# Byte places of the matmul operands in an fp32 encoder: high and low halves and low weights get begins of their own

## The chip, the core and the metric

The kernel runs on one core of a Trainium2 chip. The metric is the device time of one execution in microseconds (us). A run has three executions here, and their median is quoted.

## The reference

Two layers of a bidirectional encoder over 272 positions (16 learned ones and 256 tokens), width 2048, everything in float32. Per layer:

```
h = RMSNorm(x)
[q | k | v | f | ga | gf] = h @ W_in            # 1024, 256, 256, 1024, 2048, 2048 channels
attn    = GQA(rope(norm(q)), rope(norm(k)), v)  # 8 heads, 2 kv heads, bidirectional
fourier = Re(2-D DFT of f per group of 128 channels)
a = attn @ W_attn_br ; s = fourier @ W_four
x = x + (sigmoid(ga) * a + sigmoid(gf) * s) @ W_out
h2 = RMSNorm(x)
x = x + W_down(silu(dwconv3(h2 @ W_up_gate)) * (h2 @ W_up_val))   # 5632 channels
```

The output is the residual stream after two layers without the 16 learned positions.

## The kernel before, in words

Channels lie on the 128 partitions and positions along the free axis. Every float32 value is used as a high half, its value rounded to the format that TensorE multiplies, and a low half, the remainder. A product of two such values is three matmuls: high weights with the high moving half, high weights with the low moving half, and low weights with the high moving half. In `group` these are L248, L249 and L250, and they follow each other for every tile of 128 x 128 weights.

`group` makes two output tiles (`MG = 2`) of one projection. It walks over the input tiles `kt`; one chunk of weights holds four of these (`CW = 4`) for both outputs. `order` lists all chunks of the program, `load_raw` fetches them in that order from SyncE's queue, four ahead, and `split_w` makes `wh` (ScalarE, L193) and `wl` (VectorE, L196) of each. The tiles `wh` and `wl` have three buffers each. The keys of the groups say which projection is computed: f, k, v, q, ga, gf, a, s, o, then ug and uv (up, gate and value) and d (down). The pieces of norm, attention and Fourier work are generators that are stepped after every second weight tile.

The moving operands are kept in tiles with rows of 320 floats (`XP`) of which 272 are used. `xHL` holds the normed input, its high half in row 0 and its low half in row 1 of each `kt`; `qH` and `qL` hold the attention output for a; `mH` and `mL` hold the merged branches for o; `gHL` holds the inner activations of the feed-forward part for d. The begin inside the row is `X_AT`, `Q_AT` or `G_AT`, one number of floats per entry: `X_AT[l]` and `Q_AT[l]` by layer, `G_AT[l]` likewise.

In layer 0 all positions are computed (272 columns). In layer 1 the groups q, ga, gf, a, o and ug have 258 columns, and uv and d have 256, since the learned positions are not in the output (two more are there for the convolution). Where two halves of 256 columns fit into one bank of PSUM (512), high and low go through TensorE as one matmul of 512 columns (L244), and L245 is the low weights' matmul of 256 columns.

The code runs straight down, in the order of `order`; TensorE takes its matmuls in the order in which they were issued.

Of the kernel before, what the change touches and what calls it, by code (L numbers as in the profile page):

```python
# [10 lines left out]
F32 = mybir.dt.float32  # L11
F32R = mybir.dt.float32r
# [4 lines left out]
P = 128  # L17
# [3 lines left out]
T = NM + SEQ  # L21
# [3 lines left out]
NH = 8  # L25
# [7 lines left out]
CW = 4  # L33
MG = 2
FF_SPLIT = (24, 20)
PRE = 26
XP = 320
# [9 lines left out]
HC = 64  # L47
HC1 = HC + 1
TH = T // 2 + 2
X_AT, Q_AT, G_AT = (8, 24), (24, 40), (40, 48)  # L50
BLK = ((0, 16), (16, 144), (144, 272))

C_COS, C_SIN, C_MASK = 0, T, 2 * T
# [58 lines left out]
def encoder_kernel(ctx, tc, xT, params, consts, bmat, w_in, w_abr, w_four, w_f64, w_out, w_up, w_down, outT):  # L112
# [33 lines left out]
            k0 += n  # L146
    chunks = [ch for _, chs in order for ch in chs]
    folded = {i for i, k in enumerate(k for k, chs in order for _ in chs) if k[1] == "s"}
    st = {"raw": 0, "fetch": 0, "next": 0, "grp": 0}
    raws, splits, behind = {}, {}, {}  # L150
    RAW, LOOK = 4, 2
# [34 lines left out]

    def split_w(i, a, b, eng=None):
        if i not in splits:
            splits[i] = tuple(wp.tile([P, CW, MG * P], F32R, tag=t, name=f"{t}{i}") for t in ("wh", "wl"))
        h, lo = splits[i]  # L190
        r = raws[i]
        if eng is None:
            nc.scalar.copy(h[:, a:b], r[:, a:b])  # L193
        else:
            eng.tensor_copy(h[:, a:b], r[:, a:b])
        nc.vector.tensor_tensor(lo[:, a:b], r[:, a:b], h[:, a:b].bitcast(F32), op=ALU.subtract)  # L196
        if b == CW:
            del raws[i]
# [185 lines left out]
    nc.gpsimd.memset(remO, 0.0)  # L384

    def xs(k, half, lo=0, l=0):
        return xHL[:, k, half, X_AT[l] + lo:X_AT[l] + T]

    cos = cst[:, C_COS:C_COS + T]
    sin = cst[:, C_SIN:C_SIN + T]  # L390
# [58 lines left out]
    for l in range(DEPTH):  # L449
# [6 lines left out]

        with tc.tile_pool(name=f"mix{l}", bufs=1) as mp:
            x64 = mp.tile([96, TH], F32R, name="x64")
            E = mp.tile([P, NH, XP], F32, tag="q1", name="E")[:, :, 0:T]
            qL = mp.tile([P, NH, XP], F32R, name="qL")[:, :, Q_AT[l]:Q_AT[l] + T]  # L460
            AHn = 3 * 4 * T
            ALn = 8 * XP
            o1Hf = mp.tile([P, AHn], F32R, tag="aH", name="o1H")
# [233 lines left out]
            cnt = [0]  # L697
            for pn in pns:
                nc.gpsimd.memset(pn[:, 0:P], 0.0)
            qH = mp.tile([P, NH, XP], F32R, tag="q1", name="qH")[:, :, Q_AT[l]:Q_AT[l] + T]  # L700

            def q_stage(i, qp, qsq):
                kv, j = i // 2, i % 2
# [147 lines left out]
            for half in range(2):  # L851
                mH = mL = None
                for kind, i in BRANCH_ORDER[half]:
                    j = i - 4 * half
                    if kind == "ga":
                        tha[i] = gate("ga", i)
                    elif kind == "gf":
                        w64s.append(split_w64(l, i))
                        thf[i] = gate("gf", i)
                    elif kind == "s":  # L860
                        def s_evac(m, ps, th=thf[i]):
                            e, o = (mp.tile([P, TH], F32, tag=t, name=t) for t in ("se", "so"))
                            for a, p_ in ((e, ps[0]), (o, ps[1])):
                                nc.scalar.copy(a, p_[:, TH:2 * TH])
                                nc.vector.tensor_tensor(a, p_[:, :TH], a, op=ALU.add)
                            sp = mp.tile([P, T], F32, tag="sp", name="sp", bufs=2)
                            nc.vector.tensor_tensor(sp[:, 0:TH], e, o, op=ALU.add)
                            nc.vector.tensor_tensor(sp[:, TH:T], e[:, T - TH:0:-1], o[:, T - TH:0:-1], op=ALU.subtract)
                            t_ = th[:, m, lo:T]
                            nc.vector.scalar_tensor_tensor(t_, t_, 1.0, sp[:, lo:T], op0=ALU.add, op1=ALU.mult)  # L870

                        four_group((l, "s", i), fr, x64, w64s.pop(0), s_evac)
                    else:
                        if mH is None:
                            drain()
                            mHf = mp.tile([P, AHn], F32R, tag="aH", name="mH")
                            mLf = mp.tile([P, ALn], F32R, tag="aL", name="mL")
                            mH, mL = (t_[:, :8 * XP].rearrange("p (k t) -> p k t", k=8)[:, :, Q_AT[l]:Q_AT[l] + T] for t_ in (mHf, mLf))
                        ps = group((l, "a", i), lambda kt: (qH[:, kt, lo:T], qL[:, kt, lo:T]), W)
                        for m in range(MG):  # L880
                            k = 2 * j + m
                            t_, h_ = tha[i][:, m, lo:T], mH[:, k, lo:T]
                            nc.vector.scalar_tensor_tensor(t_, t_, 1.0, ps[m][:, :W], op0=ALU.add, op1=ALU.mult)
                            nc.vector.tensor_tensor(t_, t_, thf[i][:, m, lo:T], op=ALU.add)
                            nc.scalar.copy(h_, t_)
                            nc.vector.tensor_tensor(mL[:, k, lo:T], t_, h_.bitcast(F32), op=ALU.subtract)
                for mg in range(8):
                    ps = group((l, "o", half, mg), lambda kt: (mH[:, kt, lo:T], mL[:, kt, lo:T]), W)
                    for m in range(MG):
                        mt = 2 * mg + m  # L890
                        nc.vector.scalar_tensor_tensor(XT[:, mt, lo:T], ps[m][:, :W], 0.5, XT[:, mt, lo:T], op0=ALU.mult, op1=ALU.add)
                        if half == 1:
                            norm_in(mt, P_NF + l * KT)


        with tc.tile_pool(name=f"ffn{l}", bufs=1) as fp:
            hold = {}
            push(norm_stats(hold), 8)
            fused = 2 * W2 <= 512
            k0 = 0  # L900
            for c, n in enumerate(FF_SPLIT):
                gHL = fp.tile([P, FF_SPLIT[0], 2, XP], F32R, tag="gHL", name="gHL")[:, :, :, G_AT[l]:G_AT[l] + T]
                gH, gL = gHL[:, :, 0, :], gHL[:, :, 1, :]
                for i in range(k0 // MG, (k0 + n) // MG):
                    ps = group((l, "ug", i), xr(lo), W)
                    drain()
                    cs = []
                    for m in range(MG):
                        mt = 2 * i + m
                        wc = lambda t: prm[:, P_CW + (l * 3 + t) * FT + mt:P_CW + (l * 3 + t) * FT + mt + 1]  # L910
                        bc = prm[:, P_CB + l * FT + mt:P_CB + l * FT + mt + 1]
                        u = fp.tile([P, T], F32, tag="u", name="u", bufs=3)
                        nc.vector.tensor_tensor(u[:, lo:T], ps[m][:, :W], rstdB[:, lo:T], op=ALU.mult)
                        cv = fp.tile([P, T], F32, tag="cv", name="cv", bufs=4)
                        nc.scalar.activation(cv[:, lo2:T], u[:, lo2:T], AF.Identity, bias=bc, scale=wc(1))
                        a = max(lo2, 1)
                        nc.vector.scalar_tensor_tensor(cv[:, a:T], u[:, a - 1:T - 1], wc(0), cv[:, a:T], op0=ALU.mult, op1=ALU.add)
                        nc.vector.scalar_tensor_tensor(cv[:, lo2:T - 1], u[:, lo2 + 1:T], wc(2), cv[:, lo2:T - 1], op0=ALU.mult, op1=ALU.add)
                        nc.scalar.activation(cv[:, lo2:T], cv[:, lo2:T], AF.Silu)
                        nc.vector.tensor_tensor(cv[:, lo2:T], cv[:, lo2:T], rstdB[:, lo2:T], op=ALU.mult)  # L920
                        cs.append(cv)
                    ps = group((l, "uv", i), (lambda kt: (xHL[:, kt, :, X_AT[l] + lo2:X_AT[l] + T],)) if fused else xr(lo2), W2)
                    for m in range(MG):
                        j = 2 * i + m - k0
                        cv = cs[m]
                        val = ps[m][:, :W2]
                        if fused:
                            v = fp.tile([P, W2], F32, tag="v", name="v", bufs=2)
                            nc.scalar.copy(v, ps[m][:, W2:2 * W2])
                            nc.vector.tensor_tensor(v, v, val, op=ALU.add)  # L930
                            val = v
                        nc.vector.tensor_tensor(cv[:, lo2:T], cv[:, lo2:T], val, op=ALU.mult)
                        nc.scalar.copy(gH[:, j, lo2:T], cv[:, lo2:T])
                        nc.vector.tensor_tensor(gL[:, j, lo2:T], cv[:, lo2:T], gH[:, j, lo2:T].bitcast(F32), op=ALU.subtract)
                lastc = c == len(FF_SPLIT) - 1
                for mg in range(8):
                    two = fused and not (lastc and mg == 7)
                    ps = group((l, "d", c, mg), (lambda kt: (gHL[:, kt, :, lo2:T],)) if two
                               else (lambda kt: (gH[:, kt, lo2:T], gL[:, kt, lo2:T])), W2)
                    for m in range(MG):  # L940
                        mt = 2 * mg + m
# [62 lines left out]
```

## Time and profile before

| | |
|---|---|
| median of 3 executions | 2561.47 us (2561.24 to 2562.99) |
| profiled execution | 2561.68 us |
| its span, first to last instruction | 2559.8 us |
| TensorE, matmuls | 2552.6 us busy, 19732 matmuls |
| TensorE, weight loads | 2494.2 us busy |
| VectorE | 1690.4 us busy, 66% |
| ScalarE | 1211.4 us busy, 47% |
| GpSimd | 18.3 us busy |
| transfers | 465 MB, 57% of the 16 engines' time |
| granted TensorE clock | 0.999 of full |

A matmul's record reaches from its start to the end of its last column's way through the array, so records of successive matmuls overlap: their mean length is about 285 ns while a new one starts about every 120 ns. The distance between starts is read from the timeline.

### The profile page before, as it was taken

What the parts mean: (1) busy time and instruction counts of PE and PEld (TensorE: products, weight loads), DVE (VectorE), ACT (ScalarE), POOL (GpSimd) and SP (SyncE); (2) the same over time, 40 slices, a digit from 0 to 9 for tenths busy, and PEclk for the clock granted to TensorE, in tenths of its full rate; (3) what the DMA queues carried; (4) which work ended last, traced back from release to release, by engine and by line L of the source; (5) the groups of instructions that cost most, each with busy time, mean ns of one, the idle gap of its engine ahead of it and who ended that gap; (6) DMA issues with size and microseconds to landing.
All of it is one profiled execution on the core that took longest, in us unless ns stands there. A gap on an engine that the chain in (4) does not pass through costs nothing.

```text
span 2559.8 us, 47859 instructions
## 1 busy us (share of the span) xinstructions
PE 2552.6 (100%) x19732; PEld 2494.2 (97%) x19732; DVE 1690.4 (66%) x2691; ACT 1211.4 (47%) x1741; POOL 18.3 (1%) x37
## 2 busy tenths in 40 slices
PE   9999999999999999999999999999999999999999
PEld 9999999999999999999999999999999998999988
DVE  7687767766565446655566878677766665566654
ACT  6455434554444334444444555345554543455443
POOL 0000000000000000000000000000000000000000
PEclk9999999999999999999999999999999999999999
DMA  7555656555555555555554546666555556655565
GB/s 236 166 153 166 192 183 189 185 175 179 180 176 181 177 178 181 175 181 178 177 172 153 174 150 199 192 199 191 184 186 189 185 187 190 189 188 186 186 202 160
DMA packets 132011, 465.34 MB, mean 182 GB/s; under 512 B 15312, under 2 KB 19280, under 8 KB 131792
## 3 DMA queue, kind: packets, MB, share of 16 engines
q1 hardware_dynamic: 127424, 457.37, 56.5%
q10 hardware_dynamic: 4368, 4.92, 0.6%
q8 instruction: 154, 2.52, 0.4%
q14 instruction: 65, 0.53, 0.1%
HBM read 457.35 MB, written 2.10 MB: 179 GB/s over the span
## 4 chain that ended last, share of the span: by engine, by line
PE 98%; DVE 1%; DMA 0%; ACT 0%; issue 0%; SPq 0%; DVEq 0%; ACTq 0%
PE ps_ug L249 7%; PE ps_ug L248 7%; PE ps_ug L250 7%; PE ps_uv L244 6%; PE ps_d L244 6%; PE ps_d L249 4%; PE ps_d L250 4%; PE ps_d L248 4%; PE ps_uv L248 3%; PE ps_uv L249 3%; PE ps_uv L250 3%; PE ps_uv L245 3%; PE ps_d L245 3%; PE ps_o L249 2%; PE ps_o L248 2%; PE ps_gf L248 2%
## 5 line engine op out<-in xcount | busy, mean ns | idle before, releaser
L196 DVE TENSOR_TENSOR wl<-raw,wh 128x1024 fp32r<-128x1024 f32 (+1 forms) x835 | 1016.8, 1220 | 697.3 <-ACT wh L193 692.4
L193 ACT CAST wh<-raw 128x1024 fp32r<-128x1024 f32 (+1 forms) x834 | 871.3, 1047 | 994.4 <-PE ps_ug L249 159.5
L248 PE MATMUL ps_ug<-xHL,wh 128*128 128x272 f32 (+1 forms) x1408 | 399.6, 284 | 0.0
L249 PE MATMUL ps_ug<-xHL,wh 128*128 128x272 f32 (+1 forms) x1408 | 399.0, 283 | 0.0
L250 PE MATMUL ps_ug<-xHL,wl 128*128 128x272 f32 (+1 forms) x1408 | 399.0, 283 | 0.0
L248 PEld LDWEIGHTS ps_ug<-xHL,wh 128*128 128x128 f32 x1408 | 264.2, 188 | 0.9
L249 PEld LDWEIGHTS ps_ug<-xHL,wh 128*128 128x128 f32 x1408 | 264.2, 188 | 0.1
L250 PEld LDWEIGHTS ps_ug<-xHL,wl 128*128 128x128 f32 x1408 | 264.1, 188 | 0.0
L244 PE MATMUL ps_uv<-xHL,wh 128*128 128x512 f32 x704 | 245.0, 390 | 0.0
L244 PE MATMUL ps_d<-gHL,wh 128*128 128x512 f32 x664 | 230.3, 391 | 0.0
L249 PE MATMUL ps_d<-gHL,wh 128*128 128x272 f32 (+1 forms) x744 | 212.0, 285 | 0.0
L248 PE MATMUL ps_d<-gHL,wh 128*128 128x272 f32 (+1 forms) x744 | 212.0, 285 | 0.0
L250 PE MATMUL ps_d<-gHL,wl 128*128 128x272 f32 (+1 forms) x744 | 212.0, 285 | 0.0
L248 PE MATMUL ps_uv<-xHL,wh 128*128 128x272 f32 x704 | 200.6, 285 | 0.0
L249 PE MATMUL ps_uv<-xHL,wh 128*128 128x272 f32 x704 | 200.6, 285 | 0.0
L250 PE MATMUL ps_uv<-xHL,wl 128*128 128x272 f32 x704 | 200.6, 285 | 0.0
L245 PE MATMUL ps_uv<-xHL,wl 128*128 128x256 f32 x704 | 198.5, 282 | 0.0
L245 PE MATMUL ps_d<-gHL,wl 128*128 128x256 f32 x664 | 185.9, 280 | 0.0
L244 PEld LDWEIGHTS ps_uv<-xHL,wh 128*128 128x128 f32 x704 | 132.1, 188 | 26.9
L244 PEld LDWEIGHTS ps_d<-gHL,wh 128*128 128x128 f32 x664 | 124.2, 187 | 27.2
L248 PE MATMUL ps_ga<-xHL,wh 128*128 128x272 f32 (+1 forms) x512 | 147.5, 288 | 0.0
L248 PE MATMUL ps_gf<-xHL,wh 128*128 128x272 f32 (+1 forms) x512 | 146.3, 286 | 0.0
(284 smaller groups left out, 5891.7 us busy)
## 6 DMA issues: line engine op xcount, KB each, us to landing
raw<-in_w_up SPq DMA_DIRECT2D x352, 512.0 KB, 3.5
raw<-in_w_in SPq DMA_DIRECT2D x207, 512.0 KB, 3.6
raw<-in_w_down SPq DMA_DIRECT2D x176, 512.0 KB, 3.5
raw<-in_w_out SPq DMA_DIRECT2D x64, 512.0 KB, 3.5
raw<-in_w_four SPq DMA_DIRECT2D x32, 512.0 KB, 3.7
raw<-in_w_abr SPq DMA_DIRECT2D x32, 512.0 KB, 3.5
qs<-qp ACTq DMA_DIRECT2D x32, 68.0 KB, 4.1
outT<-ot ACTq DMA_DIRECT2D x16, 128.0 KB, 4.0
```

The source lines that it names most:

```text
L193: nc.scalar.copy(h[:, a:b], r[:, a:b])
L196: nc.vector.tensor_tensor(lo[:, a:b], r[:, a:b], h[:, a:b].bitcast(F32), op=ALU.subtract)
L244: nc.tensor.matmul(o2, h[:, c, sl], ab, start=kt == 0, stop=False)
L245: nc.tensor.matmul(o, lo[:, c, sl], ab[:, 0, :], start=False, stop=kt == nk - 1)
L248: nc.tensor.matmul(o, h[:, c, sl], a, start=kt == 0, stop=False)
L249: nc.tensor.matmul(o, h[:, c, sl], b, start=False, stop=False)
L250: nc.tensor.matmul(o, lo[:, c, sl], a, start=False, stop=kt == nk - 1)
```

## The change

All begins become pairs or tables. In bytes modulo 256 inside a partition, as the tiles are allocated:

| operand | before: high, low, wh, wl | after: high, low, wh, wl |
|---|---|---|
| layer 0: f, k, v, q, ga, gf, ug, uv, d | 32, 32, 128, 128 | 176, 48, 128, 192 |
| layer 0: a, o | 32, 32, 128, 128 | 240, 80, 128, 64 |
| layer 1: f, k, v | 96, 96, 128, 128 | 96, 160, 128, 160 |
| layer 1: q, ga, gf, a, o, ug (258 columns) | 152, 152, 128, 128 | 152, 216, 128, 192 |
| layer 1: uv | 160, 160, 128, 128 | 160, 224, 128, 128 |
| layer 1: d | 128, 128, 128, 128 | 192, 192, 128, 192 |

The three numbers for 258 columns are distances in the fourth row of the table: high weights from the high half 232 (128 - 152 modulo 256), low half from the high half 64, low weights from the high weights 64.

`X_AT`, `Q_AT` and `G_AT` now hold a (high, low) pair per layer. `WL_AT` gives the begin of the low weights inside a tile that is 64 floats longer. `both` builds the moving operand of the fused matmul of 512 columns: its two runs of 256 columns stand 336 floats apart for uv of layer 1 where they stood 320 apart. A tile `shift` of 128 bytes moves the tiles that follow it in the pool of the mixing part. No instruction is added, removed or moved: the order on each of TensorE, VectorE, ScalarE, GpSimd and SyncE, and the semaphore that each instruction waits for, are the same as before.

```diff
-X_AT, Q_AT, G_AT = (8, 24), (24, 40), (40, 48)
+X_AT, Q_AT, G_AT = ((44, 12), (24, 40)), ((44, 4), (8, 24)), ((12, 44), (0, 0))
+WL_AT = {(0, "a"): 48, (0, "o"): 48, (1, "d"): 16, (1, "k"): 8, (1, "v"): 8, (1, "f"): 8}
+WL_AT.update({(0, k): 16 for k in ("q", "k", "v", "f", "f01", "ga", "gf", "ug", "uv", "d")})
+WL_AT.update({(1, k): 16 for k in ("q", "ga", "gf", "a", "o", "ug")})
...
+    wl_at = [WL_AT.get(k[:2], 0) for k, chs in order for _ in chs]
...
-            splits[i] = tuple(wp.tile([P, CW, MG * P], F32R, tag=t, name=f"{t}{i}") for t in ("wh", "wl"))
+            h = wp.tile([P, CW, MG * P], F32R, tag="wh", name=f"wh{i}")
+            lo = wp.tile([P, CW * MG * P + 64], F32R, tag="wl", name=f"wl{i}")
+            o = wl_at[i]
+            splits[i] = h, lo[:, o:o + CW * MG * P].rearrange("p (c m) -> p c m", c=CW)
...
-        return xHL[:, k, half, X_AT[l] + lo:X_AT[l] + T]
+        return xHL[:, k, half, X_AT[l][half] + lo:X_AT[l][half] + T]
...
+            mp.tile([P, 32], F32, name="shift")
...
+            def both(t_, k, at):
+                a, n = at[0] + lo2, XP + at[1] - at[0]
+                if n == XP:
+                    return t_[:, k, :, a:a + W2]
+                b = 2 * XP * k + a
+                s = min(b, 2 * XP * t_.shape[1] - 2 * n)
+                return t_.rearrange("p k r n -> p (k r n)")[:, s:s + 2 * n].rearrange("p (r n) -> p r n", r=2)[:, :, b - s:b - s + W2]
...
-                gHL = fp.tile([P, FF_SPLIT[0], 2, XP], F32R, tag="gHL", name="gHL")[:, :, :, G_AT[l]:G_AT[l] + T]
-                gH, gL = gHL[:, :, 0, :], gHL[:, :, 1, :]
+                gHL = fp.tile([P, FF_SPLIT[0], 2, XP], F32R, tag="gHL", name="gHL")
+                gH, gL = (gHL[:, :, e, G_AT[l][e]:G_AT[l][e] + T] for e in range(2))
...
-                    ps = group((l, "uv", i), (lambda kt: (xHL[:, kt, :, X_AT[l] + lo2:X_AT[l] + T],)) if fused else xr(lo2), W2)
+                    ps = group((l, "uv", i), (lambda kt: (both(xHL, kt, X_AT[l]),)) if fused else xr(lo2), W2)
...
-                    ps = group((l, "d", c, mg), (lambda kt: (gHL[:, kt, :, lo2:T],)) if two
+                    ps = group((l, "d", c, mg), (lambda kt: (both(gHL, kt, G_AT[l]),)) if two
```

`qL`, `qH`, `mH` and `mL` are cut with the new pairs in the same way.

More of the change, by code (lines that the diff above doesn't have):

```diff
@@ L458, in encoder_kernel @@
             x64 = mp.tile([96, TH], F32R, name="x64")
+            mp.tile([P, 32], F32, name="shift")
             E = mp.tile([P, NH, XP], F32, tag="q1", name="E")[:, :, 0:T]
-            qL = mp.tile([P, NH, XP], F32R, name="qL")[:, :, Q_AT[l]:Q_AT[l] + T]
+            qL = mp.tile([P, NH, XP], F32R, name="qL")[:, :, Q_AT[l][1]:Q_AT[l][1] + T]
             AHn = 3 * 4 * T
@@ L699, in encoder_kernel @@
                 nc.gpsimd.memset(pn[:, 0:P], 0.0)
-            qH = mp.tile([P, NH, XP], F32R, tag="q1", name="qH")[:, :, Q_AT[l]:Q_AT[l] + T]
+            qH = mp.tile([P, NH, XP], F32R, tag="q1", name="qH")[:, :, Q_AT[l][0]:Q_AT[l][0] + T]
             def q_stage(i, qp, qsq):
@@ L877, in encoder_kernel @@
                             mLf = mp.tile([P, ALn], F32R, tag="aL", name="mL")
-                            mH, mL = (t_[:, :8 * XP].rearrange("p (k t) -> p k t", k=8)[:, :, Q_AT[l]:Q_AT[l] + T] for t_ in (mHf, mLf))
+                            mH, mL = (t_[:, :8 * XP].rearrange("p (k t) -> p k t", k=8)[:, :, o:o + T] for t_, o in zip((mHf, mLf), Q_AT[l]))
                         ps = group((l, "a", i), lambda kt: (qH[:, kt, lo:T], qL[:, kt, lo:T]), W)
```

## The prediction

> **What bounds the kernel now.** I read the page first: busy time, granted clock and the chain that ended last.
>
> ```profile
> span 2559.8 us, 47859 instructions
> PE 2552.6 (100%) x19732; PEld 2494.2 (97%) x19732; DVE 1690.4 (66%) x2691; ACT 1211.4 (47%) x1741; POOL 18.3 (1%) x37
> ...
> PEclk9999999999999999999999999999999999999999
> ...
> PE 98%; DVE 1%; DMA 0%; ACT 0%; issue 0%; SPq 0%; DVEq 0%; ACTq 0%
> ```
>
> TensorE is busy all the time at full granted clock, and 98% of the chain is its matmuls. No other engine sets the end. So the kernel's time is the number of matmuls times the distance from one start to the next. The change leaves number and shapes alone, so only that distance can move the time.
>
> Next the groups by line with shapes kept apart. Their mean duration is not the distance, since matmuls overlap, but the counts are exact.
>
> ```profile
> L244 PE MATMUL ps_uv<-xHL,wh 128*128 128x512 f32 x704 | 245.0, 390 | 0.0
> L244 PE MATMUL ps_d<-gHL,wh 128*128 128x512 f32 x664 | 230.3, 391 | 0.0
> L248 PE MATMUL ps_ug<-xHL,wh 128*128 128x272 f32 x704 | 200.9, 285 | 0.0
> L248 PE MATMUL ps_ug<-xHL,wh 128*128 128x258 f32 x704 | 198.6, 282 | 0.0
> L248 PE MATMUL ps_ga<-xHL,wh 128*128 128x272 f32 x256 | 74.4, 291 | 0.0
> ```
>
> L249 and L250 stand beside each L248 with the same count. Counted over all groups (the loops of the code give the same): layer 0 has 9984 matmuls of 272 columns (ug, uv and d 3x704 each, ga, gf and o 3x256 each, q and a 3x128 each, f 384, k and v 192 together). Layer 1 has 576 of 272 columns (f, k, v), 5184 of 258 columns (ug, ga, gf, a, o, q), 704 + 664 pairs of 512 + 256 columns (uv, d) and 120 of 256 (the last d group). That leaves 1132 others.
>
> The distances come from the timeline of PE, whose first column is the start. A down group of layer 0, 94 matmuls from the second row below to the row 871.49:
>
> ```profile
> 859.77 0.28 PE L250 MATMUL ps_d<-gHL,wl 128*128 128x272 f32 x1
> 859.89 0.29 PE L248 MATMUL ps_d<-gHL,wh 128*128 128x272 f32 x1
> ...
> 871.49 0.29 PE L249 MATMUL ps_d<-gHL,wh 128*128 128x272 f32 x1
> 871.61 0.28 PE L250 MATMUL ps_d<-gHL,wl 128*128 128x272 f32 x1
> 871.74 0.29 PE L248 MATMUL ps_d<-gHL,wh 128*128 128x272 f32 x1
> 871.86 0.28 PE L249 MATMUL ps_d<-gHL,wh 128*128 128x272 f32 x1
> 871.98 0.29 PE L250 MATMUL ps_d<-gHL,wl 128*128 128x272 f32 x1
> ```
>
> 11.60 us over 94 is 123.4 ns, in steps of 0.12 and 0.13. The same shape in layer 1, 46 matmuls of f:
>
> ```profile
> 1320.21 0.29 PE L249 MATMUL ps_f<-xHL,wh 128*128 128x272 f32 x1
> ...
> 1325.97 0.29 PE L250 MATMUL ps_f<-xHL,wl 128*128 128x272 f32 x1
> ```
>
> And 8 of v:
>
> ```profile
> 1378.91 0.29 PE L249 MATMUL ps_v<-xHL,wh 128*128 128x272 f32 x1
> ...
> 1379.92 0.29 PE L248 MATMUL ps_v<-xHL,wh 128*128 128x272 f32 x1
> ```
>
> 5.76 us over 46 is 125.2 ns, 1.01 us over 8 is 126.3 ns. Same operation, same columns, nothing waited for: what differs is where the operands begin. In bytes modulo 256 (64 columns) the moving operands begin at 32 in layer 0 and at 96 there; all weights at 128. So begins do cost time, and 1.8 ns is a difference already seen. The layer-1 shapes: gates of 258 columns, then ug (258) and uv (512 + 256).
>
> ```profile
> 1500.09 0.28 PE L250 MATMUL ps_ga<-xHL,wl 128*128 128x258 f32 x1
> ...
> 1500.57 0.28 PE L248 MATMUL ps_gf<-xHL,wh 128*128 128x258 f32 x1
> 1500.68 0.28 PE L249 MATMUL ps_gf<-xHL,wh 128*128 128x258 f32 x1
> ...
> 1501.16 0.28 PE L250 MATMUL ps_gf<-xHL,wl 128*128 128x258 f32 x1
> ```
>
> ```profile
> 1996.03 0.28 PE L249 MATMUL ps_ug<-xHL,wh 128*128 128x258 f32 x1
> ...
> 2006.59 0.28 PE L250 MATMUL ps_ug<-xHL,wl 128*128 128x258 f32 x1
> 2006.71 0.39 PE L244 MATMUL ps_uv<-xHL,wh 128*128 128x512 f32 x1
> 2006.94 0.28 PE L245 MATMUL ps_uv<-xHL,wl 128*128 128x256 f32 x1
> ...
> 2017.81 0.28 PE L248 MATMUL ps_ug<-xHL,wh 128*128 128x258 f32 x1
> ```
>
> Gates: 9 matmuls in 1.07 us, 118.9 ns, with single steps of 0.11. ug: 88 in 10.56 us, 120.0 ns, the same each time. uv: 32 pairs in 11.10 us, 346.9 ns. If the fixed part of a matmul is the same in ug and uv, 346.9 - 2 x 120.0 = 106.9 ns is the time of 252 columns, 0.424 ns each. Columns alone then are 115 ns of 272 and 109 of 258, so 8 to 11 ns of each matmul are not columns.
>
> What runs beside each matmul is the weight load of the next:
>
> ```profile
> 868.04 0.19 PEld L249 LDWEIGHTS ps_d<-gHL,wh 128*128 128x128 f32 x1
> 868.16 0.19 PEld L250 LDWEIGHTS ps_d<-gHL,wl 128*128 128x128 f32 x1
> 868.28 0.19 PEld L248 LDWEIGHTS ps_d<-gHL,wh 128*128 128x128 f32 x1
> ```
>
> One load follows the start of each matmul. I take the extra nanoseconds for collisions of the two reads, which depend on the difference of their begins. The rows show that begins matter; this cause they only suggest.
>
> The Trainium skill, SBUF — State Buffer, section "Who interferes with whom", gives TensorE two independent read ports, one for the moving operand and one for LDWEIGHTS, and says that it shares them with nobody. By that no begin changes anything and the sum is 0; the 123.4 against 125.2 ns speak against it.
>
> **The change part by part.**
>
> No instruction is added, removed or moved on any engine, and every wait is the same one. No stall goes, no queue is passed.
>
> *Layer 0, 272 columns, 9984 matmuls.* Before, all three of a tile's matmuls run beside a load whose begin is 96 above the moving one (128 - 32). After, the main projections have high 176, low 48, high weights 128, low weights 192: during the high matmuls the load of high weights is 208 above, during the low one the load of low weights 144 above. The a and o groups get 144 and 240. No row shows these differences. Bound below: all at the shorter of the two steps seen, 0.12: -3.4 ns x 9984 = -34 us. Bound above: the row nearest in place is ug, with 232: its 120.0 ns and 14 columns more at 0.424 give 125.9 ns, +2.5 ns x 9984 = +25 us; layer 1's v has the same shape at 126.3 ns, +2.9 ns, +29 us. I take half of the way down, 121.7 ns, -1.7 x 9984 = -17 us. Reason: equal steps 88 times running in ug, and the strict 0.12/0.13 turn of layer 0, show that a matmul meets the collision of the one before it again as long as the three have one difference; with two differences in turn the one that collides no longer repeats each time. It is a choice inside the bounds.
>
> *Layer 1 f, k, v, 576 matmuls.* The difference 32 remains for the high ones, becomes 0 for the low. From 125.2 (f) and 126.3 (v) to layer 0's 123.4: -2 to -3 ns, -1 us. Ends -3 (120) and +1 us.
>
> *258 columns, 5184 matmuls.* The difference is 128 - 152 = 232 before. After it is 232 for the high ones and 192 - 216 = 232 for the low: unchanged in every matmul. Low halves and low weights only move together by 64. I take 0. Ends: all at the 0.11 of the gates' shortest step, -8.9 ns x 3072 - 10 x 2112 = -48 us if it were held each time (it is two of nine steps now, and I give a quarter, -12 us, to the range); gates at ug's 120.0, +1.1 x 3072 = +3 us.
>
> *Pairs, 1368.* The high run of uv stays at 160, the low one goes to 224; d goes from 128 to 192 with its low weights at 192. uv and d differ by 32 bytes in begin now and by 1 ns in duration (390, 391). I take 0, and as ends half the step of 6 to 10 ns between 0.12 and 0.13, +-5 ns x 1368 = +-7 us.
>
> *The rest.* The mix pool moves by 128 bytes, half of the 256 that I count by. 512 of the 1132 other matmuls are the Fourier branch's:
>
> ```profile
> L283 PE MATMUL ps_s<-fr,wh 128*128 128x276 f32 x256 | 63.6, 334 | 0.0
> L284 PE MATMUL ps_s<-fr,wl 128*128 128x138 f32 x256 | 58.4, 228 | 0.4 <-DVE wl L196 0.4
> ...
> L196 DVE TENSOR_TENSOR wl<-raw,wh 128x1024 fp32r<-128x1024 f32 (+1 forms) x835 | 1016.8, 1220 | 697.3 <-ACT wh L193 692.4
> ```
>
> Taken at 0; ends 3 ns each way on 1132, +-3 us. VectorE writes the low weights at another begin; it is idle a third of the time and ends in time but for 0.4 us, so even some ns on each of its 835 writes stay covered. If that cover went, 10 ns each would be 8 us.
>
> Sum: -17 - 1 + 0 + 0 = -18 us against the profiled execution's 2561.68 us (span 2559.8 and 1.9 around it), which is 0.2 us above the median of 2561.47. The forecast is 2543.5 us.
>
> The Trainium skill, TensorE: Matmul & The Clock Gate, section "Back-to-back issue gap", gives an isolated warm gap of N/2.4 + 2.5 ns, 115.8 ns at 272 columns. The rows have 123.4; if the begins now freed every layer-0 matmul to that figure, the sum would be -76 us, an estimate from that page and no end of my range.
>
> **The rivals.**
>
> *Layer 0 is worse (slower).* The new differences collide in each matmul, as in layer 1's f and v. Price: from +1.8 ns (125.2) to +2.9 (126.3), +18 to +29 us, 2580 to 2591 us; with the bad ends of the others 2600. For it: of five groups read above, layer 0 has the least left over per column time (123.4 - 115.3 = 8.1 ns against 9.5 to 11), so a new place draws from worse ones. Against: its steps already show 0.12 and 0.13 in turn, so the good half exists. It decides from 0.5 ns on layer 0 (5 us).
>
> *No effect.* Begins matter only through the state that a stretch falls into, and the mean over all places is alike: within 5 us of 2561.5. For it: 258 columns keep their differences, d and uv are alike at two begins. Against: 123.4 and 125.2. The skill's rule of independent ports would give this too.
>
> *Much better.* Layer 0 all at 0.12 and 258 columns partly at 0.11: -34 - 12 - 3 = -49 us, 2512 us. For it: both steps occur. Against: nowhere are they held.
>
> **How the numbers follow.** A measurement here tells about 0.2%, 5 us. Chances: forecast (gain of 5 to 35 us) 0.42, much better 0.08, no effect 0.13, slower 0.37. So faster 0.50, same 0.13, slower 0.37. Predicted time 2543 us. Cases of both signs hold much of the chance; the forecast's own range is 2527 to 2556. The range reaches to the much better case at 2507 (2512 and 5 us of the pairs) and into the slower one to 2595 (above 2591, short of all bad ends).
>
> **What would show it.** In the changed trace, the start distances of layer 0's ug, uv and d: about 121.7 ns for the forecast, 125 to 126 for the slower rival, 123.4 for no effect. 258 columns stay at 119 to 120, pairs at 347. Split at 1320 us, where layer 1's f begins, the gain lies in layer 0 alone. A shift of some us in the 258 columns would break the rule that only the difference counts; a new wait of PE for VectorE would break the cover.

## The result, and the profile after

| | before | after |
|---|---|---|
| median of four executions | 2562.18 us (2561.24 to 2562.99) | 2530.70 us (2529.67 to 2531.18) |
| span of the profiled execution | 2559.8 us | 2529.3 us |
| ratio after to before | | 0.9877, 95% interval 0.9860 to 0.9894 |

The change makes the kernel faster by 31.5 us, 1.2%. The forecast was 2543 us, 18 us faster. (The median before has risen from 2561.47 us because a fourth execution, of 2562.89 us, is now counted in.) The page after shows the same picture as before, shorter:

```profile
span 2529.3 us, 47859 instructions
...
PE 2520.4 (100%) x19732; PEld 2462.1 (97%) x19732; DVE 1688.8 (67%) x2691; ACT 1211.1 (48%) x1741; POOL 18.3 (1%) x37
...
PE 98%; DVE 1%; ACT 0%; DMA 0%; issue 0%; SPq 0%; DVEq 0%; ACTq 0%
```

TensorE has as many matmuls, is still busy all the time, and is busy for 32.2 us less. The distances between starts are shorter. First where layer 1 begins (the first f row), in the timeline of before and then of after:

```profile
1308.58 0.29 PE L250 MATMUL ps_d<-gHL,wl 128*128 128x272 f32 x1
1308.71 0.29 PE L248 MATMUL ps_f<-xHL,wh 128*128 128x272 f32 x1
```

```profile
1299.40 0.28 PE L257 MATMUL ps_d<-gHL,wl 128*128 128x272 f32 x1
1299.52 0.29 PE L255 MATMUL ps_f<-xHL,wh 128*128 128x272 f32 x1
```

Layer 0 is 9.2 us shorter. Of the span's 30.5 us, 21.3 lie in layer 1. (The prediction put the border at 1320 us, which is inside that first f group.) Now the distances after, from the timeline: a down group of layer 0 (144 distances from the first to the last row), a ug group (96 from its first row to the uv row), the uv group behind it (32 pairs), and the down pairs of layer 1 (49 pairs).

```profile
870.16 0.29 PE L255 MATMUL ps_d<-gHL,wh 128*128 128x272 f32 x1
...
887.76 0.29 PE L255 MATMUL ps_d<-gHL,wh 128*128 128x272 f32 x1
...
1908.05 0.29 PE L255 MATMUL ps_ug<-xHL,wh 128*128 128x258 f32 x1
...
1919.07 0.28 PE L257 MATMUL ps_ug<-xHL,wl 128*128 128x258 f32 x1
1919.18 0.39 PE L251 MATMUL ps_uv<-xHL,wh 128*128 128x512 f32 x1
...
1930.28 0.29 PE L255 MATMUL ps_ug<-xHL,wh 128*128 128x258 f32 x1
...
2123.18 0.39 PE L251 MATMUL ps_d<-gHL,wh 128*128 128x512 f32 x1
...
2139.84 0.39 PE L251 MATMUL ps_d<-gHL,wh 128*128 128x512 f32 x1
```

The same 49 down pairs before:

```profile
2146.32 0.39 PE L244 MATMUL ps_d<-gHL,wh 128*128 128x512 f32 x1
...
2163.30 0.39 PE L244 MATMUL ps_d<-gHL,wh 128*128 128x512 f32 x1
```

Layer 0 stands at 122.2 ns (123.4 before), ug at 115.9 (120.0), uv at 346.9 (346.9), the down pairs at 340.0 (346.5). The distances from each start to the next, added up over both whole traces:

| part | matmuls | before, mean ns | after, mean ns | us |
|---|---|---|---|---|
| layer 0, 272 columns (without the first two groups) | 9792 | 123.3 to 130.8 by projection | 122.2 to 129.9 | -10.6 |
| layer 1, ug, 258 columns | 2112 | 120.1 | 116.1 | -8.3 |
| layer 1, q, ga, gf, a, o, 258 columns | 3072 | 118.7 to 121.2 | 115.6 to 119.1 | -8.3 |
| layer 1, d, pairs and the last group | 664 pairs, 120 | 347.2 | 340.7 | -4.7 |
| layer 1, uv pairs | 704 pairs | 346.7 | 346.7 | 0 |
| layer 1, f, k, v | 576 | 127.4 to 132.5 | 125.5 to 131.9 | -1.0 |
| first two groups and Fourier groups, both layers | 736 | | | +2.5 |

The means include the waits at a group's begin. The two d values are sums of the means of the two matmuls.

### The profile page after: what moved, and what is told of

The parts are those of the page before. It is cut to its first block, busy times and chain, and to the rows that moved or that the text cites. A ratio compares the mean times of both kernels' runs of the same rounds, so it can differ in the third digit from the quotient of the medians.

```text
span 2529.3 us, 47859 instructions
## 1 busy us (share of the span) xinstructions
PE 2520.4 (100%) x19732; PEld 2462.1 (97%) x19732; DVE 1688.8 (67%) x2691; ACT 1211.1 (48%) x1741; POOL 18.3 (1%) x37
## 4 chain that ended last, share of the span: by engine, by line
PE 98%; DVE 1%; ACT 0%; DMA 0%; issue 0%; SPq 0%; DVEq 0%; ACTq 0%
PE ps_ug L255 7%; PE ps_ug L257 7%; PE ps_ug L256 7%; PE ps_uv L251 6%; PE ps_d L251 6%; PE ps_d L257 4%; PE ps_d L255 4%; PE ps_d L256 4%; PE ps_uv L257 3%; PE ps_uv L255 3%; PE ps_uv L256 3%; PE ps_uv L252 3%; PE ps_d L252 3%; PE ps_o L255 2%; PE ps_gf L255 2%; PE ps_o L257 2%
## 5 line engine op out<-in xcount | busy, mean ns | idle before, releaser
L203 DVE TENSOR_TENSOR wl<-raw,wh 128x1024 fp32r<-128x1024 f32 (+1 forms) x835 | 1016.6, 1220 | 675.3 <-ACT wh L200 668.9
L251 PEld LDWEIGHTS ps_uv<-xHL,wh 128*128 128x128 f32 x704 | 131.9, 187 | 27.2
L251 PEld LDWEIGHTS ps_d<-gHL,wh 128*128 128x128 f32 x664 | 124.6, 188 | 26.1
```

The costliest lines, as they stand in the source:

```text
L251: nc.tensor.matmul(o2, h[:, c, sl], ab, start=kt == 0, stop=False)
```

## The experiments

I give places as in the change: three numbers, weights minus high half, low half minus high half, low weights minus high weights, modulo 256 bytes. Times of kernels that compute the encoder are medians of four or five executions, with seven or eight of the kernel before beside them; each kernel with TensorE alone was executed once. Before, layer 0 is 96, 0, 0 and the 258 columns 232, 0, 0; after, 208, 128, 64 (a and o: 144, 96, 192) and 232, 64, 64.

**Each layer alone.**

```diff
 # e1_layer0
-X_AT, Q_AT, G_AT = ((44, 12), (24, 40)), ((44, 4), (8, 24)), ((12, 44), (0, 0))
+X_AT, Q_AT, G_AT = ((44, 12), (24, 24)), ((44, 4), (40, 40)), ((12, 44), (48, 48))
 # no WL_AT entries of layer 1; "shift" in layer 0 alone
 # e2_layer1
+X_AT, Q_AT, G_AT = ((8, 8), (24, 40)), ((24, 24), (8, 24)), ((40, 40), (0, 0))
 # no WL_AT entries of layer 0; "shift" in layer 1 alone
```

> Only layer 0 has the new begins; layer 1 is as before. If the two layers' gains are separate (the start distances fell by 1.1 ns on layer 0's 9984 matmuls of 272 columns): about 11 us faster than before, less 2 us that the Fourier and first groups lost, so 2551 to 2554 us, layer 0 at 122.2 ns, layer 1's ug at 120.0 and uv at 346.7 ns as before. Rival, that the phase in which layer 0 leaves TensorE carries over into layer 1 (a running phase was seen to outlive waits): layer 1's 258 columns fall below 120 here too and the time is nearer 2540.

> Only layer 1 has the new begins; layer 0 is as before. Separate gains: 258 columns at 116 to 117 ns (-16 us), d pairs -5 us, f, k, v -1 us: 2539 to 2542 us, layer 0 at 123.4. Rival, carry-over from layer 0: layer 1 stays at 120 in part and the time is above 2548. By the rule of my prediction (only the difference of the two operands read at the same time counts) 258 columns would stay at 119 to 120 and the time would be 2555; the trace after already speaks against that.

Layer 0 alone: 2551.80 us beside 2561.28, ratio 0.9963 (0.9949 to 0.9977), -9.5 us. Layer 1 alone: 2540.86, ratio 0.9920 (0.9906 to 0.9935), -20.4 us. Together -29.9 where the whole change has -31.5. The border of the layers in the timelines, layer 0 alone first, then layer 1 alone:

```profile
1298.62 0.29 PE L254 MATMUL ps_f<-xHL,wh 128*128 128x272 f32 x1
```

```profile
1307.93 0.29 PE L254 MATMUL ps_f<-xHL,wh 128*128 128x272 f32 x1
```

In the first, layer 1's ug stays at 120.1 ns on the mean of the trace; in the second, layer 0's ug stays at 123.5 and layer 1's has 116.1. The gains are separate, and the rival of a phase carried over from layer 0 falls.

**The low weights back at their old place.**

```diff
-WL_AT = {(0, "a"): 48, (0, "o"): 48, (1, "d"): 16, ...}
+WL_AT = {}
 # and without both WL_AT.update lines
```

> High and low moving halves as in the changed kernel, all low weights at the old place. If it is the place of the moving halves alone that counts (the low half's own place): 2531 us kept, 258 columns at 116. If the low half and the low weights must move together, so that the difference stays 232 in 258 columns: ug goes back to 119 to 122 ns, layer 0 to 123 to 126, and the time is 2550 to 2590 us.

2587.75 us, ratio to before 1.0104 (1.0089 to 1.0119): 57 us slower than the whole change and 26 slower than no change. A ug group of its timeline, 96 starts:

```profile
1946.08 0.28 PE L253 MATMUL ps_ug<-xHL,wh 128*128 128x258 f32 x1
...
1957.78 0.40 PE L249 MATMUL ps_uv<-xHL,wh 128*128 128x512 f32 x1
```

That is 121.9 ns. Layer 0's ug has 124.6, the d pairs 353. At these places, moving the halves without the low weights is a loss; the moves gain only together. The numbers lie in the second of the two expected ranges. Whether its reason holds, that the difference of the two reads must stay, is tested next.

**TensorE alone.** The kernel here keeps two tiles of weights and one of moving data in place and issues stretches of the same three matmuls with begins from a table. No other engine works while they run, and the transfers are down to 1 GB/s.

```diff
+    for g, ci in enumerate(SEQUENCE):
+        kind, n, hi, lo, wh, wl = COMBOS[ci]
...
+                    nc.tensor.matmul(p[:, :n], h, a, start=kt == 0, stop=False)
+                    nc.tensor.matmul(p[:, :n], h, b, start=False, stop=False)
+                    nc.tensor.matmul(p[:, :n], l, a, start=False, stop=kt == KTN - 1)
```

> TensorE alone: 357 stretches of 48 matmuls (or 16 pairs) with operands at given byte places, each of 119 combinations three times in a shuffled order; no projection is computed and the output is not the reference's. If the extra time comes from TensorE's own two reads, the distances repeat those of the kernels within 1 ns: 272 columns with all moving at 32 and weights at 128: 123.4; 258 columns at 152: 118.7 to 120; with low half and low weights moved by 64: 116; pairs of uv 346.7, of d 346.7 before and 340.7 after; and moving all four places by the same bytes changes nothing. If it takes the other engines' or the transfers' traffic, the distances come out nearer to the columns alone, 115 and 109 ns, and no longer depend on the places.

```profile
PE 2091.6 (99%) x16560; PEld 2066.2 (98%) x16560; DVE 3.5 (0%) x9; ACT 5.2 (0%) x5; POOL 0.2 (0%) x4
```

Four stretches of 258 columns in its timeline, first and last of 48 matmuls each (L283, L284 and L285 are the three matmuls). In order of time: 232, 64, 64; then 232, 0, 0; 232, 64, 0; 232, 0, 64:

```profile
1073.48 0.28 PE L283 MATMUL ps<-mv,w 128*128 128x258 f32 x1
...
1078.97 0.28 PE L285 MATMUL ps<-mv,w 128*128 128x258 f32 x1
...
1126.40 0.28 PE L283 MATMUL ps<-mv,w 128*128 128x258 f32 x1
...
1131.98 0.28 PE L285 MATMUL ps<-mv,w 128*128 128x258 f32 x1
...
1255.17 0.28 PE L283 MATMUL ps<-mv,w 128*128 128x258 f32 x1
...
1260.85 0.29 PE L285 MATMUL ps<-mv,w 128*128 128x258 f32 x1
...
1336.22 0.29 PE L283 MATMUL ps<-mv,w 128*128 128x258 f32 x1
...
1341.83 0.28 PE L285 MATMUL ps<-mv,w 128*128 128x258 f32 x1
```

Over 47 distances that is 116.8, 118.7, 120.9 and 119.4 ns, the first tiles included. Without the first two tiles, all three repeats:

| columns, places | ns, TensorE alone | ns, kernel |
|---|---|---|
| 272: 96, 0, 0 | 123.3, 123.8, 123.3 | 123.3 (before) |
| 272: 208, 0, 0 | 124.9, 125.0, 125.0 | |
| 272: 208, 128, 64 | 122.5, 122.2, 122.2 | 122.2 (after) |
| 258: 232, 0, 0 | 118.8, 118.8, 118.6 | 118.7 to 120.1 (before) |
| 258: 232, 64, 0 | 121.4, 121.2, 122.2 | 121.9 (low weights back) |
| 258: 232, 0, 64 | 119.3, 119.4, 119.4 | |
| 258: 232, 64, 64 | 115.6, 116.2, 115.6 | 115.6 to 116.1 (after) |
| uv pairs, before and after | 347.0 to 347.1; 346.6 to 347.1 | 346.7; 346.7 |
| d pairs, before and after | 346.7, 353.1, 353.8; 340.4, 341.1, 341.1 | 346.7; 340.7 |

Most rows of the kernel are repeated within half a nanosecond. So the other engines and the transfers are not needed for the extra time; it comes with the begins of what TensorE itself reads. Two rows of before are not settled by the places: ug held 120.0 ns in every group of the kernel, where TensorE alone has 118.6 to 118.8 at the same places (and o in the kernel 118.7), and the d pairs held 346.7 where two of three stretches have 353. The rule that the time hangs on the difference of two operands read side by side falls: 232, 0, 0 and 232, 64, 64 have that difference in each matmul and lie 3 ns apart. Nor does any one move carry the gain: the low half alone costs 2.6 ns, the low weights alone 0.6, both together save 3.

**A thousand places for each shape.**

> TensorE alone, 272 columns: 992 stretches of 24 matmuls with different places (weights minus high half, low half minus high half, low weights minus high weights), every one of the 512 on a grid of 32 bytes and 480 others; no projection is computed. If the changed kernel's places are near the best that places can do, the lowest mean distance is about 121 to 122 ns (the kernel has 122.2). If the extra time can be had back by places, some triple lies at 119 or below, which would be worth 30 us in layer 0.

> The same for 258 columns. If a single difference decided, all triples with 232 as first number and equal moves of low half and low weights would agree and each first number would have one value; from the first run of TensorE alone I expect a spread of 5 ns or more inside one first number instead. If the changed kernel's 115.6 ns is near the best: lowest 115 to 116; otherwise 113 or less.

> The same for pairs of 512 and 256 columns. The pairs of d in the changed kernel take 340.4 to 341 ns, those of uv 346.7. If 340 is near the best, uv can gain 6 ns (4 us in the kernel); if lower ones exist, more. Rival: the pairs' time depends on the start and not on the places, and the lowest values are scattered without neighbours.

| | lowest | lowest 1% below | median | 95% below |
|---|---|---|---|---|
| 272 columns, 992 triples | 122.2 | 123.5 | 125.5 | 127.4 |
| 258 columns, 992 triples | 115.5 | 117.7 | 120.0 | 122.2 |
| pairs, 992 triples | 339.8 | 345.2 | 350.6 | 356.0 |

The changed kernel's 122.2 and 115.6 ns are at the lower end of all that was met, and its d pairs too. The old 123.3 of layer 0 was among the best hundredth already: a place taken at random costs 2 ns more. Of the 512 triples on the grid of 32 bytes, the eight means by the first number lie between 125.1 and 125.9 ns for 272 columns and between 119.8 and 121.0 for 258. One number says little. Each triple was tried at one place only, with the weights at 128, and once.

**More places, and repeats.**

> TensorE alone, no projection computed. 900 more random triples of 272 columns on a grid of 8 bytes, 320 of 258 columns with the low half 160 or 192 from the high one, and 13 chosen triples six times each. If 122.2 ns (272 columns) and 115.5 ns (258) are the floor of what places give, nothing below 121.5 and 115 appears; if the earlier thousand had only not met better ones, a few lie below 121. If a triple has its own time whatever came before it, the six repeats of the chosen ones lie within 1 ns of each other (3 ns for pairs); if the beginning decides, they scatter by 3 ns and more.

The lowest of 900 further triples of 272 columns is 122.2 again, twice. Six repeats of chosen ones (0, 160, 88 had a seventh stretch, of 116.5):

```
272: 208, 128, 64    122.2 122.2 122.3 122.2 122.2 122.3
258: 232, 64, 64     117.3 115.7 117.9 115.7 117.9 116.3
258: 0, 160, 88      115.5 115.6 115.5 115.5 115.5 115.5
pairs: 192, 0, 64    350.0 350.0 340.0 341.0 350.0 340.0
pairs: 192, 160, 64  352.2 352.2 349.2 340.0 340.0 351.6
```

Both expectations hold for some: some triples run alike from any beginning, others have two courses, and what ran before them picks one. 192, 0, 64 is that of the changed kernel's d. For the pairs the lowest times of the thousand are in part chance: the three places that had 340 there repeat it in one or two of six stretches.

**A version from these tables, twice.** 0, 160, 88 looked sturdier for the 258 columns than 232, 64, 64.

```diff
-X_AT, Q_AT, G_AT = ((44, 12), (24, 40)), ((44, 4), (8, 24)), ((12, 44), (0, 0))
+X_AT, Q_AT, G_AT = ((44, 12), (40, 16)), ((44, 4), (24, 0)), ((12, 44), (0, 0))
-WL_AT.update({(1, k): 16 for k in ("q", "ga", "gf", "a", "o", "ug")})
+WL_AT.update({(1, k): 44 for k in ("q", "ga", "gf", "a", "o", "ug")})
+WH_AT = {(1, k): 22 for k in ("q", "ga", "gf", "a", "o", "ug")}
 # ... begins of f, k, v and a table of the 22 uv groups
```

> The changed kernel with other places in layer 1: 258 columns at 0, 160, 88 (115.5 ns in each of six repeats), f, k, v at 240, 160, 64, and each of the 22 uv groups at another pair of numbers with the low half at 160. If the distances of TensorE alone carry over: ug 115.5 to 115.6 instead of 116.1, the gates, q, a and o 0.5 to 1.5 ns lower, -3 to -6 us; f, k, v at 124.1 to 124.4, 0; uv on the mean 349 instead of 346.7, +2 us; so 2527 to 2530 us against 2531 for the changed kernel (both beside a before of 2561 to 2562). Of the uv groups those at 192, 64 should show whether 340 is held for a whole group. Rival: the kernel's own beginnings (four matmuls from other code between the groups) put the groups into the slower courses, as 232, 64, 64 showed with 117.9: ug no lower than 116, 2531 or more.

2547.80 us, ratio to before 0.9947 (0.9931 to 0.9964): faster than before but 17 us slower than the changed kernel. Its ug group, 96 starts:

```profile
1915.91 0.29 PE L268 MATMUL ps_ug<-xHL,wh 128*128 128x258 f32 x1
...
1927.33 0.39 PE L264 MATMUL ps_uv<-xHL,wh 128*128 128x512 f32 x1
```

119.0 ns, not 115.5, and within 0.2 of that in every ug group, whatever uv group came before. It is not the beginning, then. What had changed besides the triple was that all four places had moved by 88 bytes, to a high half at 216. Of the uv groups, the one at 192, 160, 64 held 340.2 ns (31 distances from 1814.56 to 1825.10 us); the other 21 have 346.6 to 353.4. So 340 can be held for a whole uv group, though this triple has two courses above. No run gives it to all 22 groups; by these numbers that would be worth 4.6 us, an estimate.

> TensorE alone, no projection computed. First, four triples with all four places moved together by every multiple of 8 bytes. Moves by multiples of 32 changed nothing in the first run of TensorE alone; if only the three numbers count, all 32 places of a triple agree (115.5 for 0, 160, 88, and 116 for 232, 64, 64); if the absolute place counts within 32 bytes, 0, 160, 88 goes to 118.9 at the shift of 216 (24 within 32) that the last kernel used, and 115.5 comes back at multiples of 32. Second, uv pairs with high half at 160 and low half at 224, as in the changed kernel, behind its own group of 258 columns, with the weights at all 256 combinations of multiples of 16: if some weights' places suit them, some lie at 340 to 341 ns and not at 346.7; if 346 is the floor at these halves, none does.

With all four places moved together, the means by the high half's place modulo 32 (seven or eight places with two repeats each; where it says "or", the beginning picks):

| | 0 | 8 | 16 | 24 |
|---|---|---|---|---|
| 258: 0, 160, 88 | 115.5, one 117.0, one 116.5 | 115.5 to 116.6 | 117.5 to 120.0 | 118.6 to 119.3 |
| 258: 232, 64, 64 | 119.4 to 120.9 (one stretch 178.6 with a stop in it) | 116.9 or 120 to 121.3 | 119.1 to 119.9 | 115.5 or 116.3 to 117.9 |
| 272: 208, 128, 64 | 124.4 to 126.7 | 126.7 to 127.4 | 122.1 to 123.0 | 126.6 to 127.1 |
| 272: 96, 0, 0 | 123.1 to 125.2 | 124.4 to 126.9 | 123.3 to 126.7 | 126.7 to 128.9 |

The place within 32 bytes counts as well; moving all four by 32 does not. 119 is the value of 0, 160, 88 at 24 within 32. For the uv halves of the changed kernel, no weights' place among 256 gave less than 345.8.

```diff
-X_AT, Q_AT, G_AT = ((44, 12), (40, 16)), ((44, 4), (24, 0)), ((12, 44), (0, 0))
+X_AT, Q_AT, G_AT = ((44, 12), (26, 2)), ((44, 4), (42, 18)), ((12, 44), (0, 0))
+WL_AT.update({(1, k): 30 for k in ("q", "ga", "gf", "a", "o", "ug")})
+WH_AT = {(1, k): 8 for k in ("q", "ga", "gf", "a", "o", "ug", "uv")}
 # X_AT against the version above; "shift" in layer 0 alone
 # ... begins of f, k, v
```

> The changed kernel with layer 1's 258 columns at 0, 160, 88 again, but with the high half at 160, a multiple of 32 (the kernel before had it at 216, 24 within 32). If TensorE alone tells the kernel: ug at 115.5 to 115.6 (116.1 with 232, 64, 64), gates, q, a and o 0.5 to 1.5 ns lower than in the changed kernel, together -3 to -6 us; uv with weights at 160 and 128 at 346.6, 0; f, k, v at 126, +1 us: 2525 to 2529 us where the changed kernel has 2530.7. Rival, that the place within 32 bytes was not what cost the last kernel its 118.9: ug stays at 118.9 and the time is near 2545.

> The changed kernel once more, on the same chip as the one above: 2530 to 2531 us, ug at 116.1 ns.

2537.07 us, ratio to before 0.9904 (0.9887 to 0.9921); the changed kernel on the same chip 2530.08, ratio 0.9876 (0.9862 to 0.9891). The ug group of the version, 96 starts, and 27 of its d pairs:

```profile
1907.31 0.28 PE L259 MATMUL ps_ug<-xHL,wh 128*128 128x258 f32 x1
...
1918.42 0.39 PE L255 MATMUL ps_uv<-xHL,wh 128*128 128x512 f32 x1
...
2113.47 0.40 PE L255 MATMUL ps_d<-gHL,wh 128*128 128x512 f32 x1
...
2122.92 0.40 PE L255 MATMUL ps_d<-gHL,wh 128*128 128x512 f32 x1
```

ug at 115.7 ns: the place within 32 bytes was the cause, and the rival falls. But the d pairs, whose four places are those of the changed kernel, run at 350.0 instead of 340.0 in all 15 fused groups: they fell into their other course and give back 6.6 us, added over the trace. What before them decides the course is not shown. The hoped-for lower gates didn't come either (ga 119.1 as in the changed kernel, ug -0.6 us). No version run here beats the changed kernel.

## Why the prediction was right, and where it wasn't

**The bound.** Right. TensorE's starts set the time; order and waits are the same, and the gain is in the distances, but for the +2.5 us of the rest below. That begins matter was read from 123.4 against 125.2 ns, and the runs with low weights moved or not (57 us) show it outright. TensorE alone has 125.3 to 126.7 ns at the places of f, k and v before, and 123.3 to 123.8 at those of layer 0. The Trainium skill (SBUF — State Buffer, section "Who interferes with whom") has independent ports for the moving read and the weight read; that section says nothing of begins. That no begin matters, as the prediction drew from it, does not hold: with TensorE alone at work, 272 columns take from 122.2 to over 127 ns by the begins. All places moved together by 32 bytes change nothing, but distances between the operands in steps of 32 do, so how the reads lie to each other counts. Which of them meet is not separated.

**Layer 0, -17 us.** The direction was right and the size was too large: -1.1 ns, -10.6 us. The term that was mis-sized is "half of the way" to the shorter step. The reason given for it, that two differences in turn break a repeating collision, falls: 208, 128, 0 has two and layer 0's uv takes 124.4 ns with it, 96, 0, 0 has one and takes 123.3. Among the thousand places of 272 columns, the 78 triples with one difference and the 914 with two have the same median, 125.5 ns. That the direction came out right was luck. The slower rival's price was fair: low weights left behind (208, 128, 0) put layer 0 at 124.4 to 124.6 in ug, uv and d, and the first number alone at 125.0, close to its 125 to 126.

**258 columns, 0 us.** This is the step that failed: "unchanged in every matmul. Low halves and low weights only move together by 64. I take 0." It measured -16.6 us, more than half of the gain, the sign that the prediction had named as breaking its rule. The reading of what carries the cost was wrong: not the difference of the two operands read side by side, but all three numbers together and where the places lie within 32 bytes. The rule rested on too few places: each group of before had only one, with equal halves and equal weights.

**f, k, v, -1 us.** Measured -1.0. The number came out, but from the rule that fell, so it doesn't support it.

**Pairs, 0 with +-7.** uv 0 as forecast; d -4.7 us, inside the ends. The 120 unfused matmuls of the last group are in this figure.

**The rest, +-3.** Together +2.5 us, of which the Fourier groups have 1.6 and the first two groups 0.9. The first two groups wait for data and differ by 1.5 us between two executions of the changed kernel. In the Fourier groups the cover that the prediction counted on wears thin: TensorE waits there for the low weights that VectorE writes. The prediction's row of before has 0.4 us of it. After the change, and then with the low weights back at their old place:

```profile
L291 PE MATMUL ps_s<-fr,wl 128*128 128x138 f32 x256 | 58.6, 229 | 1.1 <-DVE wl L203 1.1
```

```profile
L289 PE MATMUL ps_s<-fr,wl 128*128 128x138 f32 x256 | 58.2, 227 | 0.0
```

VectorE's writes are no slower, 1220 ns on the mean in all three. The wait goes with TensorE's pace in layer 1: over all traces of the encoder it is 0 to 0.4 us where gf's mean distance is 119.6 ns or more, and 0.8 to 1.4 us where it is 117. In the slowest kernel, the one with the low weights back, the Fourier groups are 1.1 us shorter than before. All of these waits lie in layer 1, which has 0.9 of the 1.6 us; for the 0.7 in layer 0 no wait of that size is in the profile, and the cause stays open.

The sum of -18 was 13 us short: +6 from layer 0, -17 from the 258 columns, -5 from d, +2 from the rest. That the result still lies in the forecast's own range, 2527 to 2556 us, is luck: the good end of that range was layer 0 with every step at 0.12, -34 us, and layer 0 gave 10.6, while 258 columns and d, both forecast at 0, filled the rest.

**What stays open.** Why these triples are good. The three numbers, the place within 32 bytes and, for some, the beginning decide; a rule that gives the time from them was not found. The time of a stretch has to be measured, shape by shape. A version with 0, 160, 88 in layer 1 and d pairs in their faster course wasn't run, nor one with all uv groups at 340.

## What to carry to other kernels

Where TensorE is always busy with fp32 matmuls of some 260 columns and one weight load each, measure the distance between starts in the timeline and try other begins of the operands: here places were worth up to 57 us of 2560 at equal instructions. A stretch of some fifty matmuls on TensorE alone gave the kernel's distance within half a nanosecond in most rows, if the place within 32 bytes is kept, so a thousand places cost one run; a place with two courses needs repeats, and may still run otherwise in the kernel. Read a rule about two operands from a trace only if the trace has them at more than one place.

## What the runs showed that I had not expected

- Moving high half, low half and both weights together by 32 bytes changes nothing beyond what repeats at one place show, by 8 or 16 bytes up to 4.5 ns of 122 (208, 128, 64 of 272 columns: 122.2 at 16 within 32, 126.7 at 24).
- Some places have two courses that last: pairs at 192, 0, 64 take 340 or 350 ns according to what ran before, and the kernel's d groups stay in the one they begin in.
- A floor in these searches: none of 1892 triples of 272 columns was below 122.2 ns and none of 992 of 258 columns below 115.5, all with the weights at 128, so not at every place within 32 bytes. How much of these times the columns alone need is open. The prediction's estimate of 115 and 109 ns does not hold: worked out the same way from the rows after, 346.9 - 2 x 115.9 = 115.1 ns for 252 columns would make 124 ns of 272, more than the 122.2 measured. By the formula of the Trainium skill (TensorE: Matmul & The Clock Gate, section "Back-to-back issue gap") for an isolated matmul, 272 columns take 115.8 ns, an estimate; no place came near it.
